# Attention probabilities turned by 32x32 blocks on VectorE and through a DRAM scratch, 128 scores a row in the second token half, and two blocks of layer B exchanged

## The chip, the core and the metric

The kernel runs on one core of a Trainium2 chip. A core has a matrix engine (TensorE, in the profile PE, with its weight loads as PEld), VectorE (DVE), ScalarE (ACT), GpSimd (POOL) and SyncE (SP); each executes its own stream of instructions in order, and they wait for each other through semaphores. On-chip data lies in SBUF (128 partitions); TensorE writes into PSUM. Transfers from and to DRAM are issued on the queues of SP, ACT or POOL and carried out by 16 DMA engines. The metric is the device time of one execution in microseconds, lower is better; the median of several runs is given.

## What is computed

The reference is a trunk of two layers over 256 tokens of width 2048: layer A, a Mamba-2 mixer, and layer B, grouped-query attention with a sliding window of 128 tokens, one sink value per head and one shared K/V. Both are followed by a residual LayerNorm. The change touches layer B's attention alone. Cut to what matters:

```
s = einsum("bcqhrd,bckhd->bchrqk", qb, kk) * (hd ** -0.5)
qi = arange(WINDOW)[:, None] + WINDOW;  ki = arange(2 * WINDOW)[None, :]
diff = qi - ki
valid = (diff >= 0) & (diff < WINDOW) & (kpos >= 0)      # WINDOW = 128
s = where(valid, s, -inf)
m = maximum(max(s, -1), sk)                               # sk: sink of the head
p = exp(s - m);  p = p / (sum(p, -1) + exp(sk - m))
o = einsum("bchrqk,bckhd->bcqhrd", p, vv)
x = layernorm(ALPHA * x + (o * silu(gate)) @ w_out)
```

There are 32 heads of dimension 64 in 4 head groups of 8; a head group shares one K/V head. The tokens are two halves of 128. A token of the first half sees keys of the first half up to itself. A token q of the second half sees the keys of the second half up to itself, and those of the first half behind its own place: for each of the 128 places exactly one of two keys.

## The kernel before, in words

Everything is fp32. Large products are made from split numbers: a weight w is converted to wh (line 133, ACT) and the rest wl = w - wh (line 134, DVE), activations likewise, and three matmuls xH*wh, xL*wh, xH*wl replace one (`mac`, `x_stat`, `out_unit`). Weights come in units of 1 MB, each as two transfers of 512 KB on SP's queue into "wr" buffers (5), then split into "wh" and "wl" buffers (4 each). `next_unit` loads and splits two units ahead of the one that is used.

Layer A fills the first 715 us. Layer B is a list of blocks, `B_ORDER` (line 39), each of four units: ("q", j) projects the queries of head group j for both token halves (`q_block`), ("g", j) the gate (`gate_block`), ("o", j) adds head group j's part of the output projection to the residual (`out_unit`). A unit is 24 matmuls of 512 columns or 48 of 256. After each unit `tick()` counts down a list of pending steps, `later(n, fn)`: a step is placed n ticks on, so that small attention work falls between units. The order on each engine is then chosen by the scheduler of the language from program order, buffers and its own estimate of times; steps of different origin are interleaved.

`attend(j, h)` is one attention step, head group j and token half h: four q-tiles against kT give scores of 8 heads in PSUM "ax" tiles (line 804; 4 such tiles exist, 512 columns each); DVE adds a mask and brings them to SBUF as p, 128 tokens by 8 heads by nk keys, nk = 128 or 256 (809); row maxima (817), sink and negation (818 to 820), exponentials with sums on ACT, one per head (823), reciprocal and scaling (826 to 828). `turn_p`, three ticks on, transposes p on TensorE with the identity, 128x128 at a time, four into a PSUM tile (837), and ACT or DVE copies each tile to an SBUF "pt" tile (842, 844): 8 transposes for the first half, 16 for the second. `pv` multiplies v with them (851), multiplies with the gate (857) and splits the result into oH, oL (866, 867) for the output block. It stands six ticks behind `attend` in the first half, four in the second and in head group 3. `attend(j, 1)` follows `attend(j, 0)` by three ticks, by one in head group 3, and `attend(j, 0)` its q block by two.

POOL's queue in layer B carries only the bias rows of the q blocks (690), each 128 copies of a row, and near the end two rows of the norm (893, 894). At the end `out_last` runs the last output block, first for half 0, then half 1, and `done2` normalises and stores in pieces of 512 columns, with temporaries t of the "pt" tag (911, 926).

Of the kernel before, what the change touches and what calls it, by code (L numbers as in the profile page):

```python
# [57 lines left out]
def trunk(ctx: ExitStack, tc: tile.TileContext, A: dict, out: bass.AP, dbg=None):  # L58
    nc = tc.nc
# [12 lines left out]
    dram = pool("dram", space=bass.MemoryType.DRAM)  # L72
# [3 lines left out]
    def nm(s):  # L76
        uid[0] += 1
        return f"{s}_{uid[0]}"
# [11 lines left out]
    mask_a1 = cc[:, 640:896]  # L90
# [110 lines left out]
    def later(n, fn):  # L201
        pending.append([n, fn])
# [395 lines left out]
    for g in range(NG):  # L598
        t = 10 * g
# [121 lines left out]
    for h in range(2):  # L721
        ps = mm_tile()
        for ui in range(4):
            if h == 0:
                kv_u.append(next_unit())
            x_stat(ps, h, kv_u[ui], ui)
        kd = bp.tile([P, 4, 2, 64], F32, tag="qt", name=nm("kd"), bufs=2)
        nc.vector.tensor_tensor(
            kd[:, :, 0, :], ps[:, :256].rearrange("p (j d) -> p j d", j=4),
            kvb[:, :256].rearrange("p (j d) -> p j d", j=4), ALU.add,  # L730
        )
        nc.vector.tensor_tensor(vt[:, h, :], ps[:, 256:], kvb[:, 256:], ALU.add)
# [12 lines left out]

    qT = {}
    sg = {}
# [30 lines left out]
    def gate_block(j):  # L778
        t = bp.tile([P, 4, S], F32, tag="sg", name=nm("sg"), bufs=2)
        sg[j] = t  # L780
        for p_ in range(4):
# [7 lines left out]
                t[:, p_, :], t[:, p_, :], 1.0, ps[:, :S], ALU.add, ALU.mult  # L789
            )  # L790

    def attend(j, h):

        nk = P * (h + 1)
        q2 = qT[j, h]
        p = bp.tile([P, 8, nk], F32, tag=f"p{h}", name=nm("p"), bufs=1)
        mask = mask_a1 if h else mask_a0
        per = 512 // nk
        for b in range(0, 4, per):
            pss = [ax_tile(), ax_tile()]  # L800
            for i in range(per):
                for par in range(2):
                    rows = slice(64 * par, 64 * par + 64)
                    nc.tensor.matmul(
                        pss[par][:, i * nk : (i + 1) * nk], q2[rows, b + i, :], kT[rows, j, :nk],
                        start=True, stop=True,
                    )
            for par in range(2):
                nc.vector.tensor_tensor(
                    p[:, par * 4 + b : par * 4 + b + per, :],  # L810
                    pss[par][:].rearrange("p (a k) -> p a k", a=per),
                    mask.unsqueeze(1).to_broadcast([P, per, nk]), ALU.add,
                )
# [3 lines left out]
        nc.vector.tensor_reduce(mx, p[:], AX.X, ALU.max)  # L817
        nc.vector.tensor_tensor(mx, mx, sk, ALU.max)
        nc.vector.tensor_scalar(ng, mx, -1.0, None, ALU.mult)
        nc.vector.tensor_tensor(es, sk, ng, ALU.add)  # L820
        nc.scalar.activation(es, es, AF.Exp)
        for r in range(8):
            nc.scalar.activation(
                p[:, r, :], p[:, r, :], AF.Exp, bias=ng[:, r : r + 1], accum_out=rs[:, r : r + 1]
            )
        nc.vector.tensor_tensor(rs, rs, es, ALU.add)
        nc.vector.reciprocal(ri, rs)
        nc.vector.tensor_tensor(p[:], p[:], ri.unsqueeze(2).to_broadcast([P, 8, nk]), ALU.mult)

        pts = {}  # L830

        def turn_p():
            for kc in range(h + 1):
                for par in range(2):
                    pt = ax_tile()
                    for a in range(4):
                        nc.tensor.transpose(
                            pt[:, a * P : (a + 1) * P], p[:, par * 4 + a, kc * P : (kc + 1) * P], ident
                        )
                    t = bp.tile([P, 512], F32, tag="pt", name=nm("pt"), bufs=4)  # L840
                    if par:
                        nc.scalar.copy(t[:], pt[:])
                    else:
                        nc.vector.tensor_copy(t[:], pt[:])
                    pts[kc, par] = t

        def pv():
            ov = ax_tile()
            for kc in range(h + 1):
                for par in range(2):  # L850
                    nc.tensor.matmul(
                        ov[64 * par : 64 * par + 64, :], vt[:, kc, j * 64 : j * 64 + 64], pts[kc, par][:],
                        start=kc == 0, stop=kc == h,
                    )
            o = bp.tile([P, 4, P], F32, tag="o", name=nm("o"), bufs=1)
            hs = slice(h * P, (h + 1) * P)
            nc.vector.scalar_tensor_tensor(
                o[:], ov[:].rearrange("p (a t) -> p a t", a=4), 0.5, sg[j][:, :, hs], ALU.mult, ALU.mult
            )
# [12 lines left out]
        if h == 0:  # L872
            later(1 if last else 3, lambda: attend(j, 1))

# [22 lines left out]
    def done2(h):  # L897
        mv, rs = norm_scale(bp, st2, h)
        if h:

            dg = bp.tile([P, P], F32, tag="dg", name="dg")
            pss = [ax_tile(), ax_tile()]
            for c in range(2):
                sl = slice(c * 512, (c + 1) * 512)
                nc.tensor.matmul(pss[c][:], ones[0:1, :], gb2[1][0:1, sl], start=True, stop=False)
            nc.scalar.activation(dg[:], ident, AF.Copy, scale=rs[:])
            for c in range(4):
                sl = slice(c * 512, (c + 1) * 512)
                v = xr[:, h, sl]
                o = out[h * P : (h + 1) * P, sl]  # L910
                t = bp.tile([P, 512], F32, tag="pt", name=nm("t"), bufs=4)
                nc.vector.scalar_tensor_tensor(  # L912
                    t[:], v, mv[:, 0:1], gb2[0][:, sl], ALU.subtract, ALU.mult
                )
                if c < 2:
                    nc.tensor.matmul(pss[c][:], dg[:], t[:], start=False, stop=True)
                    nc.scalar.copy(v, pss[c][:])
                    nc.scalar.dma_start(o, v)
                else:
                    nc.vector.scalar_tensor_tensor(v, t[:], rs[:], gb2[1][:, sl], ALU.mult, ALU.add)  # L920
                    nc.sync.dma_start(o, v)
            return
        for c in range(4):
            sl = slice(c * 512, (c + 1) * 512)
            v = xr[:, h, sl]
            t = bp.tile([P, 512], F32, tag="pt", name=nm("t"), bufs=4)
# [100 lines left out]
```

## Time and profile before

| | |
|---|---|
| median of 3 runs | 1022.89 us (1022.04 to 1023.73) |
| span of the profiled execution | 1022.1 us |
| TensorE busy, share of the span | 1001.7 us, 98% |
| VectorE, ScalarE, GpSimd busy | 774.2 (76%), 562.8 (55%), 89.8 us (9%) |
| read from DRAM, written | 195.93 MB, 2.23 MB |
| first K/V transposes, first scores, last output block (start) | 715.0, 738.9, 984.1 us |

The profile is one execution of the program, taken by the hardware's profiler, so its durations belong to its own span of 1022.1 us and not to the median. A group of the profile is a line of the kernel with an engine, an operation and the tiles that it writes and reads; behind the count stand the busy time, the mean of one in ns, and the idle time of the engine just before, with what ended it. Matmuls are pipelined and their ends are modelled: what a series of them takes is read from start to start. A wait for several things is put down to the one that came last.

### The profile page before, as it was taken

Reading aid. Unit: us, or ns where it says so; the run is one execution under the profiler, and the core shown is the slowest. Engines: PE = TensorE matmul, PEld = TensorE weight load, DVE = VectorE, ACT = ScalarE, POOL = GpSimd, SP = SyncE. Lnnn points to the kernel's source line nnn. Section 1 sums busy time; section 2 is a strip of 40 time slices with the busy share of each in tenths; the row PEclk is TensorE's granted clock in tenths of the full one; section 3 lists DMA queues with packets and bytes.
Section 4 is the critical chain, followed back from the end, with each engine's and each line's share of the span. In section 5 each row is a group of like instructions: output and inputs, shape, how many; then the busy total and the mean of one; then the engine's idle time right before and its main releaser. Section 6 shows DMA issues by size and latency. Waiting matters only on the chain. (4 is left out here: it accounts for less than half of the span.)

```text
span 1022.1 us, 17627 instructions
## 1 busy us (share of the span) xinstructions
PE 1001.7 (98%) x7028; PEld 905.5 (89%) x7028; DVE 774.2 (76%) x1106; ACT 562.8 (55%) x924; POOL 89.8 (9%) x112
## 2 busy tenths in 40 slices
PE   7999999999999999999999999999999999999997
PEld 7999899999998998999999999868988879879975
DVE  6868887876886787696786787798577785785776
ACT  6585857637655655664663763535545453453642
POOL 0000303004003002100300300301000000000002
PEclk9999999999999999999999999999999999999999
DMA  8786676575666666656656556647655445545522
GB/s 308 249 299 246 204 245 195 171 233 169 211 218 191 218 195 204 205 188 202 208 179 218 156 190 210 227 146 232 197 167 169 156 140 183 173 140 183 194 96 82
DMA packets 57794, 199.31 MB, mean 195 GB/s; under 512 B 6304, under 2 KB 10672, under 8 KB 56944
## 3 DMA queue, kind: packets, MB, share of 16 engines
q1 hardware_dynamic: 56352, 192.14, 57.3%
q0 software_dynamic: 1072, 5.53, 1.5%
q8 instruction: 55, 0.90, 0.4%
q10 hardware_dynamic: 288, 0.52, 0.1%
q14 instruction: 27, 0.22, 0.1%
HBM read 195.93 MB, written 2.23 MB: 194 GB/s over the span
## 5 line engine op out<-in xcount | busy, mean ns | idle before, releaser
L134 DVE TENSOR_TENSOR wl<-wr,wh 128x1024 fp32r<-128x1024 f32 (+2 forms) x342 | 398.3, 1181 | 135.4 <-ACT wh L133 134.0
L133 ACT ACTIVATE wh<-wr 128x1024 fp32r<-128x1024 f32 (+2 forms) x342 | 337.4, 1011 | 238.9 <-PE mm L196 77.1
L195 PE MATMUL mm<-xH,wh 128*128 128x256 f32 x1296 | 361.2, 279 | 8.0 <-ACT wh L153 6.0
L197 PE MATMUL mm<-xH,wl 128*128 128x256 f32 x1296 | 359.8, 278 | 2.1 <-DVE wl L134 2.1
L196 PE MATMUL mm<-xL,wh 128*128 128x256 f32 x1296 | 360.1, 278 | 0.0
L195 PEld LDWEIGHTS mm<-xH,wh 128*128 128x128 f32 x1296 | 244.6, 189 | 10.2 <-ACT wh L153 6.3
L197 PEld LDWEIGHTS mm<-xH,wl 128*128 128x128 f32 x1296 | 244.5, 189 | 2.7 <-DVE wl L134 2.7
L196 PEld LDWEIGHTS mm<-xL,wh 128*128 128x128 f32 x1296 | 244.7, 189 | 1.1
L255 PE MATMUL mm<-wh,yH 128*128 128x512 f32 x256 | 101.4, 396 | 0.0
L256 PE MATMUL mm<-wh,yL 128*128 128x512 f32 x256 | 99.9, 390 | 0.0
L257 PE MATMUL mm<-wl,yH 128*128 128x512 f32 x256 | 99.7, 390 | 0.0
L492 POOL TENSOR_TENSOR yz<-yz,z 128x256 f32<-128x256 f32 x32 | 32.9, 1036 | 532.0 <-DVE yz L487 532.0
L195 PE MATMUL mm<-x1H,wh 128*128 128x256 f32 x256 | 71.9, 281 | 0.0
L197 PE MATMUL mm<-x1H,wl 128*128 128x256 f32 x256 | 71.0, 277 | 0.0
L196 PE MATMUL mm<-x1L,wh 128*128 128x256 f32 x256 | 71.0, 277 | 0.0
L359 DVE SCALAR_TENSOR_TENSOR cv<-mm,pc,cv 128x255 f32<-128x255 f32 x144 | 68.6, 476 | 1.4
L712 PE MATMUL mm<-wh,x1H 128*128 128x512 f32 x160 | 63.3, 396 | 0.0
L714 PE MATMUL mm<-wl,x1H 128*128 128x512 f32 x160 | 62.6, 392 | 0.3 <-DVE wl L134 0.2
L713 PE MATMUL mm<-wh,x1L 128*128 128x512 f32 x160 | 62.6, 391 | 0.2 <-DVE x1L L676 0.2
L255 PEld LDWEIGHTS mm<-wh,yH 128*128 128x128 f32 x256 | 48.1, 188 | 10.3 <-DVE z L429 1.0
L257 PEld LDWEIGHTS mm<-wl,yH 128*128 128x128 f32 x256 | 48.1, 188 | 10.2
L256 PEld LDWEIGHTS mm<-wh,yL 128*128 128x128 f32 x256 | 48.1, 188 | 9.0
(180 smaller groups left out, 1306.2 us busy)
## 6 DMA issues: line engine op xcount, KB each, us to landing
wr<-in_wa SPq DMA_DIRECT2D x158, 512.0 KB, 5.0
wr<-in_wo SPq DMA_DIRECT2D x64, 512.0 KB, 4.8
wr<-in_wq SPq DMA_DIRECT2D x32, 512.0 KB, 4.5
wr<-in_wg SPq DMA_DIRECT2D x32, 512.0 KB, 5.2
wr<-in_wb SPq DMA_DIRECT2D x32, 512.0 KB, 4.6
rb<-rscr SPq DMA_DIRECT2D x16, 512.0 KB, 5.4
el<-rscr SPq DMA_DIRECT2D x16, 256.0 KB, 4.8
wr<-in_wkv SPq DMA_DIRECT2D x8, 512.0 KB, 4.3
```

What stands on the lines that cost most here:

```text
L133: nc.scalar.activation(h[:, sl], raw, AF.Copy)
L134: nc.vector.tensor_tensor(l[:, sl], raw, h[:, sl].bitcast(F32), ALU.subtract)
L195: nc.tensor.matmul(ps, ah, bh, start=first, stop=False)
L196: nc.tensor.matmul(ps, ah, bl, start=False, stop=False)
L197: nc.tensor.matmul(ps, al, bh, start=False, stop=last)
L255: nc.tensor.matmul(ps[:], aH[:, k, hs], u.h[:, ks], start=k == 0, stop=False)
L256: nc.tensor.matmul(ps[:], aL[:, k, hs], u.h[:, ks], start=False, stop=False)
L257: nc.tensor.matmul(ps[:], aH[:, k, hs], u.l[:, ks], start=False, stop=k == 3)
L359: nc.vector.scalar_tensor_tensor(a[:, sft:], ps[:, : S - sft], w(3 - sft), a[:, sft:], ALU.mult, ALU.add)
L712: nc.tensor.matmul(ps[:], x1H[:, kk, hs], u.h[:, ks], start=kk == 0, stop=False)
L713: nc.tensor.matmul(ps[:], x1L[:, kk, hs], u.h[:, ks], start=False, stop=False)
L714: nc.tensor.matmul(ps[:], x1H[:, kk, hs], u.l[:, ks], start=False, stop=kk == KT - 1)
```

## The change

Six edits in layer B:

- **128 scores a row.** In the second half, p keeps for each place the one score that is valid: ACT copies the second half's keys out of PSUM, and DVE's predicated copy overwrites, where the mask is set, with the first half's. p is 128 x 8 x 128 for both halves. The score matmuls stay.
- **Turn on VectorE.** `turn_p` is one DVE transpose of the whole p in 32x32 blocks into z, then four writes on POOL's queue into a DRAM scratch (`to_dram`, one per 32 partitions, 128 KB each), arranged so that rows are keys. `load_p` reads it back as one transfer of 512 KB on POOL's queue. The transposes on TensorE and their PSUM copies are gone.
- **The second half's product.** For keys of both halves in one tile: p v0 + (p * tri)(v1 - v0), with tri the lower triangle that the mask constants hold already. DVE makes p * tri, and once, at the start, v1 - v0. The number and the size of the value matmuls stay; their moving operand is read in runs of 32 elements.
- **Places.** `turn_p` stands two ticks behind `attend`, `load_p` four, `pv` six, in head group 3 seven. The step from `attend(j, 0)` to `attend(j, 1)` stays.
- **Buffers.** p, z, the loaded tile and its product share one tag of five buffers of 4 KB a partition, in place of p0, p1 and four "pt" buffers. The temporaries of the last normalisation use the "qt" and "qT" tags.
- **Order.** ("q", 3) stands before ("o", 1) instead of behind it.

The diff, cut to its core:

```diff
-B_ORDER = [("q", 0), ("g", 0), ("q", 1), ("g", 1), ("o", 0), ("q", 2), ("g", 2), ("o", 1),
-           ("q", 3), ("g", 3), ("o", 2), ("o", 3)]
+B_ORDER = [("q", 0), ("g", 0), ("q", 1), ("g", 1), ("o", 0), ("q", 2), ("g", 2), ("q", 3),
+           ("o", 1), ("g", 3), ("o", 2), ("o", 3)]
...
+    nc.vector.tensor_tensor(vt[:, 1, :], vt[:, 1, :], vt[:, 0, :], ALU.subtract)
...
+    def to_dram(z, n, name):
+        t = dram.tile([4, P, n], F32, tag=name, name=nm(name), bufs=2)
+        for a in range(4):
+            nc.gpsimd.dma_start(
+                t[a, :, :].rearrange("(b t) f -> t b f", b=4),
+                z[32 * a : 32 * a + 32, :].rearrange("p (b f) -> p b f", b=4),
+            )
+        return t
...
-        p = bp.tile([P, 8, nk], F32, tag=f"p{h}", name=nm("p"), bufs=1)
+        p = bp.tile([P, 8, P], F32, tag="pb", name=nm("p"), bufs=5)
...
-                nc.vector.tensor_tensor(
-                    p[:, par * 4 + b : par * 4 + b + per, :],
-                    pss[par][:].rearrange("p (a k) -> p a k", a=per),
-                    mask.unsqueeze(1).to_broadcast([P, per, nk]), ALU.add,
-                )
+                v = p[:, par * 4 + b : par * 4 + b + per, :]
+                sv = pss[par][:].rearrange("p (a k) -> p a k", a=per)
+                if h:
+                    nc.scalar.copy(v, sv[:, :, P:])
+                    nc.vector.copy_predicated(
+                        v, mask_a0.bitcast(I32).unsqueeze(1).to_broadcast([P, per, P]), sv[:, :, :P]
+                    )
+                else:
+                    nc.vector.tensor_tensor(v, sv, mask_a0.unsqueeze(1).to_broadcast([P, per, P]), ALU.add)
...
         def turn_p():
-            for kc in range(h + 1):
-                for par in range(2):
-                    pt = ax_tile()
-                    for a in range(4):
-                        nc.tensor.transpose(
-                            pt[:, a * P : (a + 1) * P], p[:, par * 4 + a, kc * P : (kc + 1) * P], ident
-                        )
-                    t = bp.tile([P, 512], F32, tag="pt", name=nm("pt"), bufs=4)
-                    if par:
-                        nc.scalar.copy(t[:], pt[:])
-                    else:
-                        nc.vector.tensor_copy(t[:], pt[:])
-                    pts[kc, par] = t
+            z = bp.tile([P, 1024], F32, tag="pb", name=nm("z"), bufs=5)
+            nc.vector.transpose(
+                z[:].rearrange("p (b h q) -> p h b q", b=4, h=8), p[:].rearrange("p h (b k) -> p h b k", b=4)
+            )
+            held["d"] = to_dram(z, 256, "pd")
+
+        def load_p():
+            t = bp.tile([P, 4, 8, 32], F32, tag="pb", name=nm("pT"), bufs=5)
+            nc.gpsimd.dma_start(t[:].rearrange("p a h q -> p a (h q)"), held["d"][:].rearrange("a p f -> p a f"))
+            held["p"] = [t]
+            if h:
+                m = bp.tile([P, 4, 8, 32], F32, tag="pb", name=nm("pm"), bufs=5)
+                nc.vector.tensor_tensor(
+                    m[:], t[:],
+                    tri.rearrange("p (a q) -> p a q", a=4).unsqueeze(2).to_broadcast([P, 4, 8, 32]), ALU.mult,
+                )
+                held["p"].append(m)
...
-                        ov[64 * par : 64 * par + 64, :], vt[:, kc, j * 64 : j * 64 + 64], pts[kc, par][:],
+                        ov[64 * par : 64 * par + 64, :], vt[:, kc, j * 64 : j * 64 + 64],
+                        held["p"][kc][:, :, 4 * par : 4 * par + 4, :].rearrange("p a h q -> p h a q"),
...
-        later(3, turn_p)
-        later(4 if last or h else 6, pv)
+        later(2, turn_p)
+        later(4, load_p)
+        later(7 if last else 6, pv)
...
-                t = bp.tile([P, 512], F32, tag="pt", name=nm("t"), bufs=4)
+                t = bp.tile([P, 512], F32, tag=("qt", "qT")[c % 2], name=nm("t"), bufs=2)
```

More of the change, by code (lines that the diff above doesn't have):

```diff
@@ L89, in trunk @@
     mask_ssd = cc[:, 256:640]
-    mask_a1 = cc[:, 640:896]
+    tri = cc[:, 256:384]
     mask_a0 = cc[:, 768:896]
@@ L790, in gate_block @@
             )
+    def to_dram(z, n, name):
[6 more added lines that the diff above has]
+        return t
     def attend(j, h):
+        q2 = qT[j, h]
+        p = bp.tile([P, 8, P], F32, tag="pb", name=nm("p"), bufs=5)
         nk = P * (h + 1)
-        q2 = qT[j, h]
-        p = bp.tile([P, 8, nk], F32, tag=f"p{h}", name=nm("p"), bufs=1)
-        mask = mask_a1 if h else mask_a0
         per = 512 // nk
@@ L827, in attend @@
         nc.vector.reciprocal(ri, rs)
-        nc.vector.tensor_tensor(p[:], p[:], ri.unsqueeze(2).to_broadcast([P, 8, nk]), ALU.mult)
-        pts = {}
+        nc.vector.tensor_tensor(p[:], p[:], ri.unsqueeze(2).to_broadcast([P, 8, P]), ALU.mult)
+        held = {}
         def turn_p():
-            for kc in range(h + 1):
-                for par in range(2):
-                    pt = ax_tile()
-                    for a in range(4):
-                        nc.tensor.transpose(
-                            pt[:, a * P : (a + 1) * P], p[:, par * 4 + a, kc * P : (kc + 1) * P], ident
-                        )
-                    t = bp.tile([P, 512], F32, tag="pt", name=nm("pt"), bufs=4)
-                    if par:
-                        nc.scalar.copy(t[:], pt[:])
-                    else:
-                        nc.vector.tensor_copy(t[:], pt[:])
-                    pts[kc, par] = t
+            z = bp.tile([P, 1024], F32, tag="pb", name=nm("z"), bufs=5)
[14 more added lines that the diff above has]
+                held["p"].append(m)
         def pv():
@@ L925, in done2 @@
             v = xr[:, h, sl]
-            t = bp.tile([P, 512], F32, tag="pt", name=nm("t"), bufs=4)
+            t = bp.tile([P, 512], F32, tag=("qt", "qT")[c % 2], name=nm("t"), bufs=2)
             nc.vector.scalar_tensor_tensor(
```

## The prediction

> **What bounds the kernel now.** I first asked the windows view for the stretch in which layer B works, from the first score block to just before the last output block. Columns: start and end, length, then busy time of PE, PEld, DVE, ACT and POOL, the granted clock, the DMA share and GB/s.
>
> ```profile
> core 0 of [0], span 1022.1 us
> core 0: us, PE busy (x) PEld busy (x) DVE busy (x) ACT busy (x) POOL busy (x), PEclk, DMA share, GB/s
> 716.00:984.00 268.00, 266.89 (x1673) 227.17 (x1671) 191.80 (x297) 135.20 (x281) 2.13 (x4) 1.00 0.51 171
> ```
>
> TensorE (PE) is busy for 266.89 of 268.00 us at full clock; VectorE (DVE) has 76 us free, ScalarE (ACT) 133, POOL nearly all, the DMA engines half. Busy PE alone proves little, so I next read who waits for whom there (total, times, longest).
>
> ```profile
> ACT wh L133 <- PE mm L196: 23.2, 7, 4.5
> ACT wh L133 <- PE mm L713: 22.4, 6, 4.1
> DVE sm L826 <- ACT p L823: 16.5, 8, 4.0
> ```
>
> The weight conversion on ACT waits for PE to give weight buffers back, not PE for the conversion. Work taken off PE's stream in this stretch therefore comes off the end, one for one, as long as no new wait replaces it. The third row serves later: DVE already stands idle for up to 4.0 us in each attention step, and PE does not feel it.
>
> **The transposes that leave PE.** PE's timeline (start, duration, line, count, idle before) shows what they cost. A matmul's duration overlaps the next one, so I take start to start.
>
> ```profile
> 811.02 1.03 PE L837 MATMUL ax<-cc,p 128*128 128x128 f32 x8
> 811.99 2.71 PE L804 MATMUL ax<-kT,qT 64*128 64x256 f32 x16
> ...
> 832.18 1.97 PE L837 MATMUL ax<-cc,p 128*128 128x128 f32 x16
> 833.90 0.49 PE L712 MATMUL mm<-wh,x1H 128*128 128x512 f32 x1
> ...
> 953.33 2.00 PE L804 MATMUL ax<-kT,qT 64*128 64x256 f32 x16
> ...
> 966.29 1.04 PE L837 MATMUL ax<-cc,p 128*128 128x128 f32 x8
> 967.08 0.47 PE L255 MATMUL mm<-wh,oH 128*128 128x512 f32 x1
> ...
> 973.72 1.53 PE L837 MATMUL ax<-cc,p 128*128 128x128 f32 x12
> 976.22 0.66 PE L837 MATMUL ax<-cc,p 128*128 128x128 f32 x4 [0.96 <-DVE o L857]
> 976.63 0.48 PE L255 MATMUL mm<-wh,oH 128*128 128x512 f32 x1
> ```
>
> Eight transposes take 811.99 - 811.02 = 0.97 us, sixteen 833.90 - 832.18 = 1.72. Head groups 0 to 2 run alike: 3 x (0.97 + 1.72) = 8.1. Head group 3 takes 0.79 and 2.91 (with a 0.96 us wait for a PSUM buffer): 3.7. All 96 together: 11.8 us.
>
> VectorE: DVE Perf Modes in the Trainium skill (The three transpose paths; Rules for kernel authors) speaks against the move: it sends a 128x128 transpose to TensorE where PSUM output is acceptable, at about 390 ns in bf16, since DVE turns only 32x32 blocks. Taken as time on the path, 390 ns x 96 would be 37 us, and the sum below would end near 984; the rows say 0.11 to 0.12 us each, and the rows decide, both on the size and on the engine to relieve.
>
> **What the missing transposes do to the scores.** The second half's scores take 2.71 us right behind transposes, but 2.00 at 953.33, where none is ahead of them: they wait for the four PSUM "ax" buffers that the transposes hold. Three such places give 3 x 0.71 = 2.1 back. In the new order, attention (3,1) lands on the same tick as the value products of (2,1); their buffer plus four for scores make five. The nearest row is the 0.96 wait just quoted; I charge 0.7. Net gain 1.4, between 1.1 and 2.1.
>
> **PE work that stays.** Score and value matmuls keep their number and shapes. The value product's moving operand is now read in runs of 32 elements. No row shows such a read on PE: nothing at one end, a doubling at the other (rival c). I take nothing: 32 fp32 elements in a row are long against one.
>
> **DVE and ACT.** Rows of the groups view (count | busy, mean ns | idle before), same stretch, first DVE, then ACT:
>
> ```profile
> L809 DVE TENSOR_TENSOR p<-ax,cc 128x512 f32<-128x512 f32 x24 | 15.3, 679 | 1.3 <-PE ax L804 1.3
> ...
> L828 DVE TENSOR_TENSOR p<-p,sm 128x2048 f32<-128x2048 f32 x4 | 9.2, 2290 | 0.1
> L817 DVE TENSOR_REDUCE sm<-p 128x8 f32<-128x2048 f32 x4 | 9.1, 2284 | 0.1
> L844 DVE COPY pt<-ax 128x512 f32<-128x512 f32 x12 | 8.1, 680 | 0.0
> ```
>
> ```profile
> L823 ACT ACTIVATE p<-p,sm 128x256 f32<-128x256 f32 x32 | 15.8, 496 | 21.8 <-DVE sm L819 21.8
> ...
> L823 ACT ACTIVATE p<-p,sm 128x128 f32<-128x128 f32 x32 | 12.4, 388 | 16.6 <-DVE sm L819 16.6
> L823 ACT ACTIVATION_READ_ACCUMULATOR p<-p,sm 128x1 f32 x64 | 12.0, 187 | 0.0
> L842 ACT COPY pt<-ax 128x512 f32<-128x512 f32 x12 | 6.5, 574 | 0.0
> ```
>
> DVE loses 16 of the mask additions (16 x 0.68 = 10.9), half of L828 and L817 in the second half (4.6 each) and L844 (8.1): 28.2. It gains 16 predicated copies of 256 elements (0.34 each by half of L809's time, at most 0.68: 5.4 to 10.9), eight block transposes of 1024 elements (1.15 each by half of L828, at most its 2.29: 9.2 to 18.3), four products with the triangle (4 x 1.15 = 4.6) and one small subtraction: 19 to 34. Net -9 to +6 against 76 us free. ACT loses 6.5 and 32 x 0.108 = 3.5 and gains 16 copies of at most 0.574 (9.2). Neither engine becomes the bound; price on the path 0. Were the cover gone, DVE's +6 would be the cost.
>
> **The round trip through DRAM.** Each of the eight attention steps now issues four writes of 128 KB and one load of 512 KB on POOL's queue, all in 1 KB runs. The queue otherwise holds the bias rows and, at the end, the norm's rows; it is in order, so a late write holds the load behind it, and with it the value product that PE has next in its own order. First the cover, in the second half of head group 0, the tighter kind since the product with the triangle comes on top:
>
> ```profile
> 757.44 2.79 PE L804 MATMUL ax<-kT,qT 64*128 64x256 f32 x16
> ...
> 785.06 1.94 PE L851 MATMUL ax<-pt,vt 128*64 128x512 f32 x8
> ```
>
> ```profile
> 769.79 2.28 DVE L828 TENSOR_TENSOR p<-p,sm 128x2048 f32<-128x2048 f32 x1
> ```
>
> From the end of these scores (760.23) to L851 lie four weight units, the first half's value product (1.0, half of the 1.94) and sixteen transposes (1.72): (785.06 - 760.23 - 2.7) / 4 = 5.5 us a unit. The value product now stands six units behind the scores instead of four: 2.0 + 6 x 5.5 = 35 us after their start. The probabilities are ready 769.79 + 2.28 - 757.44 = 14.6 us after that start; halved L817 and L828 take off 2.3, shorter exponentials 8 x 0.108 = 0.9, and copy plus predicated copy cost about what the mask did: 11.4. Cover: 35 - 11.4 = 23.6 us.
>
> What has to fit, from the DMA view (queue rows: packets, MB, share of 16 engines; issues with KB and median us to landing) and the POOL row of the groups view:
>
> ```profile
> q1 hardware_dynamic: 11803, 42.96, 48.3%
> q0 software_dynamic: 448, 2.62, 2.7%
> ```
>
> ```profile
> el<-rscr SPq DMA_DIRECT2D x16, 256.0 KB, 4.8
> ...
> rscr<-f SPq DMA_DIRECT2D x2, 64.0 KB, 3.5
> ```
>
> ```profile
> L690 POOL DMA_DIRECT2D bias<-in_qb x3 | 1.6, 537 | 69.6 <-DVE qt L761 68.9 <-DVE vt L732 0.7
> ```
>
> Transpose 1.15 to 2.3; four issues at 0.54, the fourth begun after 1.6, its landing 3.5 (a 64 KB write) to 4.8; the load's issue 0.54 (a row of 128 pieces) to 2.1 (four times the pieces); its landing 4.8 (el, the same 1 KB runs, half the bytes) to 9.6; the triangle product 1.15. Sum: 13.2 to 21.6 us against 23.6. It fits at both ends, by 2 to 10 us; I take 16 us, nearer the el row. The shared tag of five buffers holds four tiles of one step and the next scores; the sixth waits for the preceding value product at worst, half a unit before it is wanted: nothing. First halves need no triangle product; head group 3 waits seven units and has 5.5 us more. The cover is why I charge nothing; beyond it every microsecond late is a microsecond of PE.
>
> For the weight stream: 8.4 MB more is 7.5% of the engines by the bytes of q1; by q0's mean packet, 2.7% of 268 us x 16 over 448 = 0.26 us, the 8192 new ones would be 50%. On top of 51% the first leaves room, the second would not. q0's packets carry 5.8 KB each, the new ones 1 KB, so I take the first. Cost 0; at the other end weights come late.
>
> **Order of blocks, and the tail.** q3 moves ahead of o1, and with it its weight loads on SP's queue, its bias row on POOL's and its splits on ACT and DVE: the same count, in the same steps of a unit. Each output block still finds its head group's values at least two units old; the last value product lies two units before the last output block. Removing the transposes also removes one separate visit of PE to the attention work in head group 3. The last block and the normalisation only change the buffers that four temporaries use. All 0.
>
> **Sum.** 11.8 + 1.4 = 13.2 us off the profiled execution: 1022.1 - 13.2 = 1008.9 for its span. The three runs lie between 1022.04 and 1023.73, median 1022.89, so that execution is at their low end; off the median: **1009.7 us**. About 0.2%, 2 us, is what a measurement of this kernel can tell from no change.
>
> **Rivals.**
> (a) DVE blocks itself. The triangle product is queued on DVE behind a load; weight splits and PSUM evictions stand behind it. If it is queued right behind the load's issue, DVE stands for issue and landing, 5.3 to 11.7 us, at four places; up to 4.0 is shown to be free (L826), so PE would lose 1.3 to 7.7 each. At 2 each: 1009.7 + 8 = 1017.7; from 3.3 each on the gain is gone. For it: DVE is in order. Against: DVE's stream in the trace interleaves splits with attention work, so a later place is likely. Chance 0.14.
> (b) Slower: descriptors on POOL. 40 transfers are prepared by an engine that before did almost nothing, and if each issue stretches fivefold beside DVE's work (2.7 us, the load's 2.7 to 10.7), the trip becomes 1.15 + 4 x 2.7 + 3.5 + 2.7 + 4.8 + 1.15 = 24 to 32 us. The place is L851 in head groups 0 to 2, six times. It decides from 23.6 + 13.2 / 6 = 25.8 us; at 28 it costs 6 x 4.4 = 26: 1036. For it: no row has forty such issues beside DVE. Against: L690's issues keep to 0.537 us on average with DVE busy 191.80 of 268. Chance 0.11. SBUF — State Buffer in the Trainium skill (SBUF: two separate sides) has a cause for it: descriptors for POOL's queue are written through a port that DVE in its two-port modes holds shut; whether the new one-input transposes count among these, no run here shows.
> (c) The value product reads its runs at half rate: 1.94 for a second half, about 1.0 for a first, 4 x 2.9 = 11.8 in all, so 1009.7 + 11.8 = 1021.5, no change. For it: untried here. Against: each run is 128 contiguous bytes. Chance 0.07. That leaves 0.68 for the forecast.
>
> **Range and chances.** The forecast's own range is 1007 to 1013: downward the full 2.1 for the scores and the spread of the runs (0.85), upward a few stalls under 1 us. To hold 8 in 10 the range reaches into (a), to 1019; (b), (c) and the dear end of (a) stay outside. Faster: 0.68 and 0.12 of (a). Same: (c) and 0.01 of (a). Slower: (b) and 0.01 of (a).
>
> **What would show it.** Right: L837 gone from PE; PE busy above 99% in layer B; the visit of second-half scores at 2.0; L851 with idle time near zero in all eight steps; load landings at 5 to 10 us; the last output block starting 13 us earlier; the end of the program after it unchanged. Rival (a): idle on DVE at the triangle product, released by a DMA, and PE waiting for wl soon after. Rival (b): idle on PE ahead of L851, released by that load, and POOL issues well over 0.54 us. Rival (c): eight L851 taking near 4 us instead of 1.94. If PE is as busy as before and the end is not 10 us earlier, the reading of the bound is wrong.

## The result and the profile after

| | before | after |
|---|---|---|
| median | 1022.75 us (4 runs, 1022.04 to 1023.73) | 1007.98 us (4 runs, 1006.79 to 1008.46) |
| span of the profiled execution | 1022.1 us | 1005.9 us |
| layer B, K/V transposes to last gain broadcast (both starts) | 296.6 us | 283.2 us |

The ratio is 0.9855, 95% interval 0.9841 to 0.9869: faster by 14.8 us (13.4 to 16.3). Forecast were 13.2 us off and 1009.7.

First the windows view of the changed kernel, over nearly the same work as the 268 us that the prediction quoted (columns as there).

```profile
716.00:970.00 254.00, 253.89 (x1573) 214.97 (x1572) 184.59 (x298) 128.57 (x282) 25.73 (x44) 1.00 0.64 211
```

The stretch is 14 us shorter and TensorE is as full as before. No long wait took the place of the 96 transposes. POOL went from 2.13 to 25.73 us, the DMA share from 0.51 to 0.64.

PE's timeline of the changed kernel (start, duration, line, count, idle before) gives the ends of layer B, two second-half score visits and the value products:

```profile
712.30 1.03 PE L739 MATMUL ax<-cc,kd 128*128 128x128 f32 x8
...
753.82 2.00 PE L814 MATMUL ax<-kT,qT 64*128 64x256 f32 x16
...
792.30 1.08 PE L869 MATMUL ax<-pT,vt 128*64 128x512 f32 x4
...
917.78 1.03 PE L869 MATMUL ax<-pm,vt 128*64 128x512 f32 x4
918.74 2.00 PE L814 MATMUL ax<-kT,qT 64*128 64x256 f32 x16
...
953.62 1.08 PE L869 MATMUL ax<-pT,vt 128*64 128x512 f32 x4
954.62 0.50 PE L255 MATMUL mm<-wh,oH 128*128 128x512 f32 x1
...
995.50 1.98 PE L925 MATMUL ax<-gb,cc 1*128 1x512 f32 x4
```

The same two ends in the kernel before:

```profile
715.02 1.03 PE L739 MATMUL ax<-cc,kd 128*128 128x128 f32 x8
...
1011.59 1.98 PE L905 MATMUL ax<-gb,cc 1*128 1x512 f32 x4
```

Layer B takes 995.50 - 712.30 = 283.2 us instead of 1011.59 - 715.02 = 296.6: 13.4 less, which is the change. The other 2.7 us by which layer B starts earlier lie in code that did not change. Over the 13 traces of this case whose layer A is the same, layer B starts between 712.30 and 715.12, and at 714.26 where the changed kernel was measured again (below). So this first profile flatters the change a little. The last output block (the last 96 matmuls of its lines) starts at 973.64 instead of 989.74; the 984.1 of the table before is one unit ahead of it. From there to the end of the span it is 32.3 us after and 32.4 before.

No value product of the eight steps has idle time in brackets before it (rows of three are shown). The scores of the second half take 2.00 at each place, where 2.71 was quoted before. Start to start over all eight visits, the scores take 12.07 us instead of 14.29.

What was new, in DVE's and POOL's groups of the changed kernel (count | busy, mean ns | idle before and its releasers):

```profile
L848 DVE STREAM_TRANSPOSE z<-p 128x1024 f32<-128x1024 f32 x8 | 9.9, 1236 | 0.0
L842 DVE TENSOR_TENSOR p<-p,sm 128x1024 f32<-128x1024 f32 x8 | 9.8, 1221 | 0.1
...
L823 DVE COPY_PREDICATED p<-cc,ax 128x256 f32<-128x256 int32 x16 | 5.8, 435 | 0.0
L859 DVE TENSOR_TENSOR pm<-pT,cc 128x1024 f32<-128x1024 f32 x4 | 4.9, 1226 | 23.7 <-issue 15.0 <-DMA pT<-pd 8.7
```

```profile
L797 POOL DMA_DIRECT2D pd<-z x32 | 17.5, 554 | 150.7 <-DVE z L848 150.7
L855 POOL DMA_DIRECT2D pT<-pd x8 | 6.1, 757 | 43.0 <-DMA pd<-z 23.8 <-ACT oH L885 7.0 <-DMA wr<-in_wb 6.4
```

A block transpose of 1024 elements a partition takes 1.236 us, about the same as a multiplication of that size. DVE stands idle for 23.7 us in all before its four triangle products. PE feels it once, at the longest of the four. These are rows of DVE and of PE's weight loads (PEld):

```profile
955.01 1.23 DVE L859 TENSOR_TENSOR pm<-pT,cc 128x1024 f32<-128x1024 f32 x1 [8.48 <-issue]
```

```profile
957.75 0.19 PEld L255 LDWEIGHTS mm<-wh,oH 128*128 128x128 f32 x1 [0.53 <-DVE sg L789]
```

A gate step on DVE (`sg`, line 789) that hands a PSUM buffer back to PE stands behind the product and starts at 957.29. The output block waits for that buffer, and one of its units takes 6.1 us (954.62 to 960.72) where the same unit takes 5.7 in the repeat of this kernel, whose DVE stood idle there for 5.0 us.

Who waits for whom (total, times, longest), against the rows of before:

```profile
ACT wh L133 <- PE mm L196: 15.8, 5, 4.2
DVE pm L859 <- issue: 15.0, 2, 8.5
```

The weight conversion still waits for PE to give buffers back, now 15.8 us where it was 23.2: PE is the bound with somewhat less in hand behind it. The DMA view (queue: packets, MB, share of the engines; issue: count, KB, median us to landing):

```profile
q0 software_dynamic: 3136, 11.01, 11.9%
...
wr<-in_wb SPq DMA_DIRECT2D x32, 512.0 KB, 5.7
...
pd<-z POOLq DMA_DIRECT2D x32, 128.0 KB, 5.3
pT<-pd POOLq DMA_DIRECT2D x8, 512.0 KB, 6.9
```

One round trip, the second half of head group 0, from DVE's and POOL's timelines:

```profile
766.19 1.24 DVE L848 STREAM_TRANSPOSE z<-p 128x1024 f32<-128x1024 f32 x1
...
782.69 1.23 DVE L859 TENSOR_TENSOR pm<-pT,cc 128x1024 f32<-128x1024 f32 x1 [5.13 <-DMA pT<-pd]
```

```profile
767.72 2.19 POOL L797 DMA_DIRECT2D pd<-z  x4 [8.45 <-DVE z L848]
...
775.62 0.75 POOL L855 DMA_DIRECT2D pT<-pd  x1 [1.63 <-ACT oH L885]
```

The load lands at 782.50. From the transpose's start to the product's end it is 783.92 - 766.19 = 17.7 us. PE wants the result at 792.30 (the value product above): 8.4 us to spare. Over all eight steps the trip to the load's landing takes 15.4 to 18.6 us, and the spare time is 4.5 to 12.1 us.

### The profile page after: what moved, and what is told of

Read it like the earlier page. It is cut to its first block, busy times and chain, and to the rows that moved or that the text cites. A ratio compares the mean times of both kernels' runs of the same rounds, so it can differ in the third digit from the quotient of the medians.

```text
span 1005.9 us, 17518 instructions
## 1 busy us (share of the span) xinstructions
PE 989.1 (98%) x6932; PEld 893.6 (89%) x6932; DVE 767.8 (76%) x1107; ACT 557.5 (55%) x928; POOL 114.5 (11%) x152
## 4 chain that ended last, share of the span: by engine, by line
PE 75%; DVE 9%; DMA 6%; issue 4%; ACT 4%; POOL 1%; SPq 0%; DVEq 0%; ACTq 0%; POOLq 0%
PE mm L195 13%; PE mm L196 13%; PE mm L197 13%; PE mm L255 7%; PE mm L256 6%; PE mm L257 6%; PE mm L712 3%; PE mm L713 3%; PE mm L714 3%; DVE wl L134 3%; DMA wr<-in_wa 2%; DVE cv L359 1%; ACT wh L133 1%; PE ax L476 1%; PE ax L814 1%
## 5 line engine op out<-in xcount | busy, mean ns | idle before, releaser
L257 PEld LDWEIGHTS mm<-wl,yH 128*128 128x128 f32 x256 | 48.1, 188 | 10.2
```

The lines of the kernel that those rows point to most:

```text
L257: nc.tensor.matmul(ps[:], aH[:, k, hs], u.l[:, ks], start=False, stop=k == 3)
```

## The experiments

My theory: PE's stream is the bound; the gain is the transposes' own time start to start and the score waits that they caused; everything else lies under cover of about 24 us. Rival theories: the exchanged blocks make the gain; the narrower scores make it; DVE's load, POOL's queue or the DMA traffic take a part of it away.

### e1_order_only: the new order alone

```diff
-B_ORDER = [("q", 0), ("g", 0), ("q", 1), ("g", 1), ("o", 0), ("q", 2), ("g", 2), ("o", 1),
-           ("q", 3), ("g", 3), ("o", 2), ("o", 3)]
+B_ORDER = [("q", 0), ("g", 0), ("q", 1), ("g", 1), ("o", 0), ("q", 2), ("g", 2), ("q", 3),
+           ("o", 1), ("g", 3), ("o", 2), ("o", 3)]
...
-        later(4 if last or h else 6, pv)
+        later(7 if last else 4 if h else 6, pv)
```

The edits are made in the kernel before; its transposes stay on PE.

> The kernel before with the new order of blocks alone; for head group 3 the value product stands seven ticks behind its scores, as the order asks. Theory (the gain is TensorE time that left the stream): the same matmuls and transposes in another order, so 1022.7 us, within 2 either way. Rival (the order gives part of the gain, by mending a wait at the end of the list): under 1019.

Measured 1021.57 against 1023.36, ratio 0.998 (0.9968 to 0.9992): 1 to 3 us faster. The median lies within the 2 us that the theory allowed. PE's timeline:

```profile
950.12 1.91 PE L837 MATMUL ax<-cc,p 128*128 128x128 f32 x16
951.78 0.36 PE L195 MATMUL mm<-x1H,wh 128*128 128x256 f32 x1
```

The sixteen transposes of head group 3 now take 951.78 - 950.12 = 1.66 us, not 2.91: the 0.96 wait is gone. Layer B is 1.0 us shorter. So the order isn't the gain. What it gives alone in this trace is a wait that goes with the transposes in any case.

### e2_narrow_pe: 128 scores a row, the turn stays on PE

```diff
-            for kc in range(h + 1):
-                for par in range(2):
...
+            for par in range(2):
...
+                    nc.tensor.transpose(pt[:, a * P : (a + 1) * P], p[:, par * 4 + a, :], ident)
...
+                if h:
+                    m = bp.tile([P, 512], F32, tag="pt", name=nm("pm"), bufs=4)
+                    nc.vector.tensor_tensor(
+                        m[:].rearrange("p (a q) -> p a q", a=4), t[:].rearrange("p (a q) -> p a q", a=4),
+                        tri.unsqueeze(1).to_broadcast([P, 4, P]), ALU.mult,
+                    )
+                    pts[1, par] = m
```

The kernel before gets the change's copy, predicated copy and v1 - v0 as well: 64 transposes remain of 96.

> The kernel before with 128 scores a row alone: copy and predicated copy, half the maxima, exponentials and scaling in the second half, the triangle product; TensorE turns the probabilities as before, but 64 blocks instead of 96. Theory: only the 32 missing transposes count, 32 x 0.109 = 3.5 us, at most 1.5 more from waits for PSUM: 1017.7 to 1019.3. Rival (VectorE and ScalarE relieved are worth time): this edit takes off nearly all that the whole change takes off them, so at least half of the gain, 1015 or less.

Measured 1018.56, ratio 0.996 (0.9948 to 0.9971): 4.1 us faster. Layer B is 4.6 us shorter, which is 32 transposes at 1.72 / 16 = 0.11 us (3.5) and the 0.96 wait. The narrower scores pay through the transposes that they save, as the theory has it.

### e3_unread_turns: the change, with 96 transposes put back on PE

```diff
         def turn_p():
+            for kc in range(h + 1):
+                for par in range(2):
+                    pt = ax_tile()
+                    for a in range(4):
+                        nc.tensor.transpose(pt[:, a * P : (a + 1) * P], p[:, par * 4 + a, :], ident)
             z = bp.tile([P, 1024], F32, tag="pb", name=nm("z"), bufs=5)
```

Nobody reads the 96 results.

> The changed kernel with 96 transposes of the probabilities on TensorE put back, whose results nobody reads or copies. Theory: TensorE's stream is the bound, so they cost their time start to start, 96 x 0.109 = 10.5 us, up to 13 with waits for PSUM: 1018.5 to 1021. Rival (the gain came from copies, masks or the order): 1008 to 1011.

Measured 1021.87, ratio 0.9995 (0.9981 to 1.0009): the gain is gone. PE's group:

```profile
L851 PE MATMUL ax<-cc,p 128*128 128x128 f32 x96 | 11.8, 273 | 1.8 <-DVE p L842 1.8
```

Layer B is 12.4 us longer than the change's: 8 transposes take 0.79 and 16 take 1.66 start to start, and PE waits 1.8 us for p. This is the strongest single result: PE time put back comes back on the end. It also prices a transpose in place: with all 96 put back, the whole kernel is 13 to 14 us slower. VectorE: DVE Perf Modes in the Trainium skill (The three transpose paths) gives 390 ns for a 128x128 transpose in bf16 on TensorE, which as an estimate would be 37 us for 96; the measurement decides.

### e4_order_before: the change, with the blocks in their old order

```diff
-B_ORDER = [("q", 0), ("g", 0), ("q", 1), ("g", 1), ("o", 0), ("q", 2), ("g", 2), ("q", 3),
-           ("o", 1), ("g", 3), ("o", 2), ("o", 3)]
+B_ORDER = [("q", 0), ("g", 0), ("q", 1), ("g", 1), ("o", 0), ("q", 2), ("g", 2), ("o", 1),
+           ("q", 3), ("g", 3), ("o", 2), ("o", 3)]
```

> The changed kernel with the order of blocks of before. Theory: in head group 3 only five units lie between the second half's scores and the last output block, 27.5 us, against 11.4 + 16 to 18 us that the probabilities and their round trip need, and the gate product, the split and the other half's value product come on top with nothing to cover them: 4 to 10 us of TensorE, 1012 to 1018. Rival (the order does not matter): 1007 to 1009.

Measured 1021.44, ratio 0.9975 (0.9962 to 0.9987). Against the change's 1007.98 and 1009.26 that is 12 to 13 us lost, more than the 4 to 10 expected. PE's timeline and its windows:

```profile
973.02 1.08 PE L869 MATMUL ax<-pT,vt 128*64 128x512 f32 x4 [0.46 <-DMA pT<-pd]
...
978.84 1.98 PE L869 MATMUL ax<-pT,vt 128*64 128x512 f32 x4 [4.74 <-DMA pT<-pd]
```

```profile
978.84:980.84 2.00, 2.00 (x5) 0.39 (x5) 2.00 (x3) 0.46 (x2) 0.00 (x0) 0.50 0.04 8
...
986.84:988.84 2.00, 2.00 (x6) 1.52 (x6) 1.02 (x2) 1.62 (x2) 0.00 (x0) 0.50 0.00 0
988.84:990.84 2.00, 2.00 (x10) 1.64 (x9) 0.20 (x1) 0.29 (x1) 0.00 (x0) 0.95 0.00 0
```

The load of the last attention step lands too late for its place, PE stands for 4.74 us, and then the granted clock (the column behind POOL) is 0.50 for 10 us, in which half the work is done: 5 us more. The four broadcasts of the norm's gains also stand ahead of the last product here (at 980.74), where the change runs them behind the last output unit; at full clock they are about 2 us. Waits of 5.2, the clock's 5 and these 2 make 12.2 of the 12.3 us by which the stretch from the K/V transposes to the last output matmul is longer than in e0_after_again. The price of the wait was expected at one for one, and that was too low.

### e0_after_again: the change once more

The kernel is the change, unedited, run beside the following ones.

> The changed kernel again, unaltered, beside the kernel before, for a second reading of its ratio. Theory: 13.2 to 14 us of layer B, ratio 0.9865, 0.985 to 0.988; layer A ends within 2.5 us of where it ends before, either way, since nothing in it is changed. Rival (part of the 14.8 us first measured lies in layer A for good): layer A ends over 2 us earlier in this profile too.

Measured 1009.26 against 1023.28, ratio 0.9862 (0.9844 to 0.988). Its layer B takes 282.8 us, 13.8 less than before's; the start of layer B is at 714.26.

### e5_pv_five and e5_pv_four: the cover made smaller

```diff
-        later(4, load_p)
-        later(7 if last else 6, pv)
+        later(3, load_p)
+        later(7 if last else 5, pv)
```

and the same with 4 in place of 5. The value products of head groups 0 to 2 then stand five or four units behind their scores.

> The changed kernel with the value product five ticks behind the scores, the load placed at three, in head groups 0 to 2. Theory (a cover that still fits costs nothing): the first halves' cover of 30.6 us stands against 28 to 29 needed, the second halves' 31.3 against 29.2 to 30.8; both fit by 0.5 to 2.5 us, so 1008 to 1012 with an occasional short wait, where four ticks gave 15 us of waits in the profile. Rival (the cost grows evenly with each tick taken away): halfway to the 1032 of four ticks, about 1020.

> The changed kernel with the value product four ticks behind the scores instead of six, and the load placed at three, in head groups 0 to 2. Theory (beyond its cover each microsecond of the round trip is one of TensorE): from the changed kernel's trace, scores to landing or triangle product take 28 to 31 us, the new cover is 25 us; first halves wait 2.9, 3.8 and 3.1 us, second halves, whose cover those waits lengthen, 2.1, 1.9 and 0.9: 14.7 in all, so 1020 to 1026. Rival (the scheduler or another queue hides it): 1007 to 1011.

With five units 1009.82, ratio 0.9872 (0.9857 to 0.9886): a unit of 5.5 us less cover costs nothing that can be told. With four units 1032.05, ratio 1.0079 (1.0052 to 1.0106), 22.8 above e0_after_again. The waits, a timeline row and two windows of four units:

```profile
PE ax L869 <- DMA pT<-pd: 15.0, 6, 3.4
...
PE ax L869 <- DVE pm L859: 0.4, 2, 0.3
```

```profile
765.27 1.98 PE L869 MATMUL ax<-pT,vt 128*64 128x512 f32 x4 [3.19 <-DMA pT<-pd]
```

```profile
765.27:767.27 2.00, 2.00 (x5) 0.39 (x5) 0.00 (x0) 0.00 (x0) 0.00 (x0) 0.50 0.03 8
767.27:771.27 4.00, 4.00 (x15) 3.25 (x16) 3.95 (x7) 1.58 (x2) 0.00 (x0) 0.83 0.00 0
```

The waits make 15.4 us, near the 14.7 expected in all. The rest is the clock after three of them: 2 us at 0.50 and 4 at 0.83 lose 1.7, the place after a wait of 3.42 us loses 4 x (1 - 0.61) = 1.6, and the one after 3.08 us (0.69, 0.50 and 0.96 in three stretches of 2 us) loses 1.7. Together 20.4 of the 21.2 us by which layer B is longer than in e0_after_again (304.0 and 282.8). So the cover is real, its edge lies between five and four units, and beyond it a late microsecond costs more than one.

### e6_sp_queue: the forty transfers on SP's queue

```diff
-            nc.gpsimd.dma_start(
+            nc.sync.dma_start(
```

The same is done for the load.

> The changed kernel with the 40 DRAM transfers of the probabilities issued on SyncE's queue, among the weight loads, instead of GpSimd's. Theory (the cover has 5 to 9 us to spare and weights are loaded two units ahead): no change against the changed kernel, ratio to before 0.984 to 0.988. Rival (one queue in order makes weights wait for the writes to land): TensorE waits for converted weights in each attention step, 1013 or more.

Measured 1009.43, ratio 0.9857 (0.9841 to 0.9872), the same as e0_after_again. It does not matter here which of the two queues carries the trip, nor that the weights share it.

### e8_q_too: the queries turned the same way

```diff
-                    nc.tensor.transpose(
-                        pt[:, p_ * P : (p_ + 1) * P], qf[:, p_ * P : (p_ + 1) * P], ident
-                    )
...
+                nc.vector.transpose(
+                    z[:].rearrange("p (b q c) -> p c b q", b=4, c=4),
+                    qf.rearrange("p (c b k) -> p c b k", c=4, b=4),
+                )
+                qd = to_dram(z, 128, "qd")
+                q2 = bp.tile([P, P, 4], F32, tag="qT", name=nm("qT"), bufs=2)
+                nc.gpsimd.dma_start(
+                    q2[:].rearrange("p (a q) c -> p a (q c)", a=4), qd[:].rearrange("a p f -> p a f")
+                )
...
-                        pss[par][:, i * nk : (i + 1) * nk], q2[rows, b + i, :], kT[rows, j, :nk],
+                        pss[par][:, i * nk : (i + 1) * nk], q2[rows, :, b + i], kT[rows, j, :nk],
```

The attention steps are moved to give this trip time too.

> The changed kernel with the queries turned in the same way: one VectorE transpose, four writes and one load per half, the scale moved into the keys, attention two ticks later, its halves one or two ticks apart. 32 transposes leave TensorE. Theory: 32 x 0.109 = 3.5 us less, less what strided weight loads cost (the queries now lie four apart; no run shows it): 1003 to 1006. Rival (the cover, now with two round trips one behind the other, is used up): stalls at the scores or the value product, 1009 or more.

Measured 1013.24, ratio 0.9903 (0.9885 to 0.9921): 4 us slower than the change where 3 to 6 faster was expected. PE waits for nothing in layer B; the price stands in the weight loads of the score matmuls, here and (second fence) in e0_after_again:

```profile
L817 PEld LDWEIGHTS ax<-kT,qT 64*128 64x128 f32 x128 | 15.6, 323 | 2.4 <-issue 1.2 <-PE mm L256 0.4 <-PE mm L713 0.4
```

```profile
L814 PEld LDWEIGHTS ax<-kT,qT 64*128 64x128 f32 x128 | 9.8, 187 | 3.1 <-issue 1.2 <-PE mm L713 0.7 <-PE mm L256 0.4
```

With every fourth element read, a load of stationary data takes 323 ns instead of 187. The scores take 16.96 us start to start instead of 12.07, so 4.9 are added where 32 transposes saved 3.2. That is 1.7 us of the 4. The profiled execution took 1010.44; why the others took up to 1015.91 is open.

### e10_q_packed: the queries turned, then packed

```diff
-                q2 = bp.tile([P, P, 4], F32, tag="qT", name=nm("qT"), bufs=2)
+                w = bp.tile([P, 4, 4, 32], F32, tag="pb", name=nm("qw"), bufs=5)
...
+                q2 = bp.tile([P, 4, P], F32, tag="qT", name=nm("qT"), bufs=2)
+                nc.scalar.activation(
+                    q2[:].rearrange("p c (a q) -> p c a q", a=4), w[:].rearrange("p a c q -> p c a q"),
+                    AF.Copy, scale=0.125,
+                )
```

The diff is against e8_q_too: ACT copies the loaded queries into contiguous rows.

> The queries turned through DRAM as well, but packed by a copy on ScalarE after the load, so that the weight loads of the scores are contiguous again. Theory (the strided weight loads ate the gain of the earlier attempt, 4.9 us in its profile): scores back at 12.1 us in all, end about 4 us before the changed kernel's in the profile, 1004 to 1007. Rival (two round trips one behind the other leave no cover, and the timed executions stall now and then): 1010 to 1014 again.

Measured 1025.54, ratio 1.0026 (1.0012 to 1.0041): slower than before the change. The waits:

```profile
ACT qT L777 <- DMA qw<-qd: 36.1, 8, 10.3
...
PE ax L875 <- DMA pT<-pd: 10.6, 1, 10.6
...
PE ax L820 <- ACT qT L777: 6.1, 1, 6.1
```

The scores are back at their old lengths, but ACT, which converts the weights, now stands behind the query loads for 36.1 us. PE waits once for queries, 6.1 us, and once for probabilities, 10.6; that two trips in series overran the cover fits this, but what made that one load late is open.

### e9_layer_a: layer A's inputs turned the same way

```diff
+        for i in range(4):
+            nc.vector.transpose(
+                zv[:, i, :, :, :].rearrange("p c b q -> p c b q"),
+                st.xs[i][:].rearrange("p (c b q) -> p c b q", c=2, b=4),
+            )
...
+        if g:
+            at(t + 6, turn_xs, g)
+            at(t + pos["y"], tr_loaded, g)
+        else:
+            at(t + pos["tr"], tr, g)
```

This takes 56 of 64 transposes off PE in layer A, with a scratch, four writes and a load for each of seven groups.

> The changed kernel with the same method for layer A: the inputs of head groups 1 to 7 are turned on VectorE, written to DRAM and read back, where TensorE turned them; 56 of 64 transposes leave its stream, 56 x 0.109 = 6.1 us, with their visits 7. About six units, 33 us, lie between the last input and its use, less 4 for its convolution, against a round trip of 15 to 19. Theory (it fits here as in layer B): 1002 to 1005. Rival (layer A's DMA engines and VectorE have no room, or VectorE stands behind the loads): 1008 or more.

Measured 1008.75, ratio 0.9857 (0.9844 to 0.987): no measurable gain over the change. The transposes left PE (6.33 us start to start became 0.79), but waits came in; of this kernel and then of e0_after_again, layer A:

```profile
PE ax L708 <- DVE xr L703: 4.2, 2, 3.9
PE mm L195 <- DVE cv L359: 2.0, 2, 1.1
PE mm L197 <- DVE wl L134: 1.7, 1, 1.7
```

```profile
PE ax L670 <- DVE xr L665: 2.2, 2, 1.9
PE mm L195 <- ACT wh L133: 1.0, 1, 1.0
PE mm L197 <- DVE wl L134: 0.8, 1, 0.8
PE mm L195 <- DVE cv L359: 0.7, 2, 0.4
```

With the small rows left out these are 7.9 us, all for DVE, against 4.7: 3.2 more. The 13 traces with the old layer A have 3.5 to 5.4. After the 3.9 us wait the clock falls to 0.84, 0.50 and 0.81 over three stretches of 2 us, 1.7 us more. So about 5 of the 5.5 us are given back. In layer A, where PE already waits on DVE, the same step does not pay; that the waits come from DVE's added 6.5 us in this stretch (523.5 against 517.0 busy) was not tested by itself. No version that was run beats the change measurably.

### e11_four_turns: each transpose on DVE four times

```diff
-            nc.vector.transpose(
+            for _ in range(4):
+                nc.vector.transpose(
```

> The changed kernel with each VectorE transpose executed four times, 24 more of 1.24 us each, 30 us more on VectorE and 3.7 us more on each round trip. Theory (VectorE has about 70 us free in layer B, and the cover 4.5 to 9 us to spare): 1008 to 1011. Rival (VectorE or the trip is at its limit): 1015 or more.

Measured 1019.16, ratio 0.9964 (0.995 to 0.9978): most of the gain is gone, where nearly nothing was expected to be. DVE's timeline and the waits:

```profile
749.54 1.24 DVE L849 STREAM_TRANSPOSE z<-p 128x1024 f32<-128x1024 f32 x1
...
755.53 1.24 DVE L849 STREAM_TRANSPOSE z<-p 128x1024 f32<-128x1024 f32 x1
```

```profile
PE ax L870 <- DMA pT<-pd: 5.3, 3, 4.2
PE ax L768 <- DVE qt L705: 2.6, 2, 1.6
```

DVE still has 54 us free in the 254 from 716 on (200.45 busy). But other work goes between the four, so they take 756.77 - 749.54 = 7.2 us, and later steps of DVE are late: PE waits 5.3 us for loads, 2.6 for queries, and runs at half clock after the longest wait (value products of 4 in 1.97 instead of 1.03). The waits and the slow clock make 9.9 of the 10.4 us by which layer B is longer than in e0_after_again. That free time was the wrong measure; what counts is how late the work in the chain comes.

## Why the prediction was right, point by point

- **The bound.** Right. PE is full after the change as before it, and work put back on PE (e3_unread_turns) comes back at the end.
- **Transposes, 11.8 us.** Right: they are gone, and in e3_unread_turns they cost 12.4 us with a wait of 1.8 in it.
- **Scores, net 1.4.** Gained were 2.2 us. The 0.7 charged for attention (3,1) did not appear: at 918.74 its scores stand right behind the value product and take 2.00. In its place came the 0.4 us that the output block from 954.62 loses behind DVE. So -11.8 - 2.2 + 0.4 = -13.6, measured -13.4. That the sum was so close to the forecast's 13.2 is in part luck, since the loss came from another place than the one charged.
- **The value product's read, nothing.** Right: 11.51 us start to start before and after. Rival (c) is out. The same liberty on the stationary side has a price (e8_q_too).
- **DVE and ACT, nothing on the path.** Right for the change: DVE's net is 184.59 - 191.80 = -7.2 us, inside -9 to +6; transposes 1.236 at the low end of 1.15 to 2.29, predicated copies 0.435 inside 0.34 to 0.68. But the reason, 76 us free, was poor: e11_four_turns had 54 free in 254 us and lost 10 us of the gain.
- **The round trip, 16 us under a cover of 23.6.** In the second halves, with the product, it is 16.7 to 19.9 us, inside 13.2 to 21.6 but longer than taken. (The low terms add up to 12.7, not 13.2; nothing hangs on it.) At the place that was worked out 8.4 us are to spare where the sum left 7.6, but both terms were about 2 us short: the trip took 17.7, and the time from its start to the value product is 26.1. Landings of the loads took 5.6 to 8.5 us, inside 5 to 10. The step to five units costs nothing.
- **DMA, 7.5% more.** q0 went from 2.7 to 11.9%, 9.2% more. The rule by bytes was right and its sum wrong: 8.4 x 48.3 / 42.96 is 9.4. The packets were not as taken either: 2688 more, of 3.1 KB, not 8192 of 1 KB. The output blocks' weights land in 5.7 us instead of 4.6, and no wait of PE for them shows in layer B.
- **Order of blocks, 0.** As a term of the sum it held: the 1.0 us of layer B that the exchange gives alone (e1_order_only) is the 0.96 wait, which the 11.8 holds already. The account of it was incomplete. Without the exchange the change loses 12 to 13 us (e4_order_before): the last step's trip needs the block that the exchange puts between. I counted what the blocks issue, not what cover they give.
- **"Beyond it every microsecond late is a microsecond of PE".** Too low. Nine waits of 3.08 to 10.64 us were, with one exception, followed by a halved clock.
- **Rival (a).** Its mechanism was there, DVE standing 3.6 to 8.5 us before each triangle product. Its price was 0.4 us once, behind the 8.5, not 1.3 to 7.7 at each of four places. The repeat has stands of 3.3 to 6.7 us and no such loss, so the free limit lies above the 4.0 us that the trace of before could show.
- **Rival (b).** Issues take 554 and 757 ns, not 2.7 us, and moving them to SP's queue changes nothing (ratio 0.9857). The port conflict that SBUF — State Buffer in the Trainium skill (SBUF: two separate sides) describes does not show with these transposes.
- **The base.** I put the profiled execution at the low end of the runs. A run is 1.8 us above its span (1007.71 and 1005.9 after), so the span of 1022.1 belongs to a run near 1023.7, the high end. The forecast was taken off the median and did not depend on it.

## What to carry to other kernels

Where the matrix engine is the bound, price a step on it by start to start in the trace, and move it, even by a trip through DRAM of 16 to 20 us, if that many microseconds of other matrix work lie between maker and user. Work out this cover for the last step of a chain as well as for the first, and count what the order of blocks gives to it. Free time of an engine says little; look at what queues behind a waiting instruction, and remember that the same move paid in layer B and not in layer A or for the queries.

## What the runs showed of the hardware

- After PE had waited 3.08, 3.19, 3.42, 3.91 and 4.23 us, the clock record of the traces has the granted clock at 0.50 for 3.4 us each time. At waits of 4.74 and 6.07 us it is 10.2 us, and at 10.64 us 13.7, part of which lies within the last two waits. One wait of 3.17 us was followed by 1.00, and so were all 21 waits of 1.24 to 1.91 us between 80 and 950 us. At the program's start, and once in e5_pv_five (1.14 and 0.76 us, at 63 us), shorter waits close together were followed by 0.50. Nothing here fixes a rule.
- Reading moving data in runs of 32 elements cost TensorE nothing; loading stationary data with a step of four elements cost 323 instead of 187 ns.
- A DMA issue on POOL took 554 ns with 128 KB and 757 ns with 512 KB.
